# A float32 transformer layer on one core: the order of two subtractions in the gate units, and two output tiles moved to the end in halves

## The chip, the cores and the metric

The kernel runs on one core of one Trainium2 chip. The metric is the device time of one execution in microseconds. An execution's own time is a little longer than its span in the profile, which runs from its first to its last instruction.

## The reference, cut to what matters

One layer on 512 tokens of width 1024, all in float32: a feed-forward block, a token mixer (two kinds of attention), a second feed-forward block, and a final norm. The change lies in the two feed-forward blocks and in the final norm.

```python
def rmsnorm(x, g):
    y = x32 * lax.rsqrt(jnp.mean(x32 * x32, axis=-1, keepdims=True) + EPS)
    return y * g

def swiglu(x, w_gate, w_up, w_down):          # d_ff is 2816
    return (jax.nn.silu(x @ w_gate) * (x @ w_up)) @ w_down

x = x + 0.5 * swiglu(rmsnorm(x, ffn1_norm), ...)
x = x + token_mixer(rmsnorm(x, mix_norm), ...)
x = x + 0.5 * swiglu(rmsnorm(x, ffn2_norm), ...)
return rmsnorm(x, final_norm)
```

## The kernel before

**Layout.** Everything is transposed: x is eight tiles x0 to x7 of 128 features by 512 tokens. A "half" is 256 tokens, `left` or `right`. To keep float32 precision each operand is split into a high part (a cast to fp32r, on ScalarE) and a low part (the rest, by a subtraction on VectorE), and each product is three matmuls: high x high, high x low, low x high (`mm3`, lines 123 to 125 of the profile).

**Units and steps.** The two blocks are called a and b in tile names (`pygb` is bank y of a gate unit in block b). Most of a block is a list `units`, worked in order:

- `g` and `u`: two rows of gate (or up) columns at once, by a seven-product scheme after Strassen and Winograd. Its steps, in the order of `SEVEN`, are `a11` to bank w, `s3` to z, `s2` to x, `a12` to w, `s1` to y, `a22` to x, `s4` to y. A step is 12 matmuls, 256 wide.
- `p`: a plain product of one output tile with the first six rows of the activations (`PLAIN`), 18 matmuls 512 wide, added to x.
- `d`: a down unit, again seven steps, for two output tiles and eight rows; there are two groups of four.

In both blocks the list runs: gate and up units, five plain tiles (0 to 4), the first down group, more gate and up units, three plain tiles (5 to 7), the second down group. The final norm follows block b.

**Banks.** A step's partial sum is seeded from another bank (ScalarE copies w to x, then x to y). In a gate unit, after `s1`, bank y plus p7 (a half tile that ScalarE copied out of bank z into `res["bc"]`, called `rbc_n` in the profile) is one half of the second row; after `a22`, bank x plus p7 is the other. `s4` accumulates into bank y again, so it must come after the first of these adds. The adds are line 414 of the profile (`second_row`), and they write into tile `g1`; a Silu (line 495) follows in place. The first row comes from banks w and y by a Silu each (line 476) into tile `g0`. Both tiles are from a pool of two buffers (`ptb`), so a new pair's g0 and g1 take the buffers of the pair before.

**What happens to a finished pair.** After the up unit, `kept` forms the combinations that the down units need and splits them. The last two splits are `t0_rest` (h4 from g0 and h3) and `t1_rest` (h6 from g1 and h5), subtractions on VectorE, line 526. They are the last readers of the old g0 and g1.

**What sets the order.** On TensorE, VectorE and ScalarE the order is written out by hand, on SP and POOL too: the planner `pipeline` puts every small task on a heap with a due time and a rank. Due times are counted in `STEP` (1410 ns, one step) and `PLAIN_STEP` (4080 ns); tasks are issued in order of due time, rank and entry, and each engine works its own instructions strictly in that order. For a step at time t, its cast is due at t - 4 steps, its subtraction at t - 3 (line 386; `total`, lines 364 and 366, adds up two weights for `s2` and `s4`), its product at t. The results of a step are handled when the next starts.

**Weights.** `load` brings a unit's weight rows to one of three raw buffers through SP. `weight_sums` makes two sums of weight blocks: SP loads one block to a slot, and POOL issues a second, accumulating transfer on top. It is due 14 steps ahead, and not before the slot is free. In group 0 the down units use slots 8 to 11 in turn, in group 1 slots 8 to 11 and then 0 to 3.

**The end.** The last down unit (tiles 6 and 7) has `LAST_SEVEN`: steps `a22` and `s1` change places, so that the left halves of both tiles are done one step earlier. `last` squares the finished halves; `final_means` sums squares over features with one-column matmuls (line 1229) and makes the reciprocal root (lines 1232 to 1240); `final_spread` spreads the scale over partitions with a matmul (line 1244); `final_out` multiplies the eight tiles of a half by gain and scale (line 1254) and stores them, mostly in pairs (lines 1257, 1259). The left half's means stand ahead of the last step; its spread and one pair of outputs follow that step, then the right half's means, the other three left pairs, the right half's spread and its outputs.

Of the kernel before, what the change touches and what calls it, by code (L numbers as in the profile page):

```python
# [44 lines left out]

SEVEN = (("a11", "w", "b11"), ("s3", "z", "t3"), ("s2", "x", "t2"), ("a12", "w", "b21"),
         ("s1", "y", "t1"), ("a22", "x", "t4"), ("s4", "y", "b22"))
LAST_SEVEN = SEVEN[:4] + (SEVEN[5], SEVEN[4], SEVEN[6])

PAIR_SLOTS = ((6, 7, 16, 17, 18, 19, 20), (28, 29, 30, 31, 32, 33, 21),  # L50
              (34, 35, 36, 37, 38, 39, 40), (41, 42, 12, 13, 43, 14, 15))
GROUP_SUMS = (((8, 9), (10, 11), (8, 9), (10, 11)), ((8, 9), (10, 11), (0, 1), (2, 3)))


STEP, PLAIN_STEP = 1410, 4080
HS = S // 2
ODD = 8
F32_MAX = 3.4028234e38
# [6 lines left out]
def tile_macaron(ctx: ExitStack, tc, xs, xT, wf, wgu1, wst1, wd1, wdg1, wqk, wv, wo, wgu2, wst2, wd2,  # L65
# [132 lines left out]
    def ffn(wgu, wst, wd, wdg, n0, n1, norm, early, res, nm, hooks, ended, first=None,  # L198
# [96 lines left out]
        units = [("g", n1)]  # L295
        for j in range(n1 + 2, PLAIN + 8, 2):
            units += [("g", j), ("u", j)]
        units += [("p", m) for m in range(5)] + [("d", 0, m) for m in range(0, KD, 2)]
        for j in range(PLAIN + 8, JF, 2):
            units += [("g", j), ("u", j)]  # L300
        units += [("p", m) for m in range(5, KD)] + [("d", 1, m) for m in range(0, KD, 2)]
        ops, begin, starts, now = [], {}, [], 0
        for u in units:
            begin[u] = len(ops)
            seven = LAST_SEVEN if last is not None and u == units[-1] else SEVEN
            for o in (("p",),) if u[0] == "p" else seven:
                ops.append((u, o))
                starts.append(now)
                now += PLAIN_STEP if u[0] == "p" else STEP
        starts.append(now)  # L310

        def rows(u):
# [4 lines left out]

        def sum_slots(u):
            if u[0] == "d":
                return GROUP_SUMS[u[1]][u[2] // 2]  # L320
            if u == units[0]:
                return PAIR_SLOTS[0][:2]
            if u[1] == PLAIN + 8:
                return GROUP_SUMS[0][u[0] == "u"]
            o = 2 if u[0] == "g" else 4
            return PAIR_SLOTS[(u[1] - PLAIN) // 2 % 4][o:o + 2]

# [12 lines left out]

        def load(u):
            raws[u] = []
            whole = [wd[u[1]]] if u[0] == "p" else [rows(u)[0], rows(u)[1][:, 512:]]
            for a in whole:
                t = wp.tile([P, 1024], F32, tag="raw", name=f"raw{len(raws[u])}{nm}{u[0]}")
                nc.sync.dma_start(t[:, :a.shape[-1]], a)
                raws[u].append(t)

        def source(t):
            u, o = ops[t]  # L350
            r0 = raws[u][0]
            if o[0] == "p":
                return r0[:, :PLAIN * P]
            return {"a11": r0[:, :512], "a12": r0[:, 512:], "a22": raws[u][-1][:, :512],
                    "s1": sums[u][0][:], "s3": sums[u][1][:], "s2": second.get(u),
                    "s4": second.get(u)}[o[0]]
# [10 lines left out]

        def high(t):
            u, o = ops[t]
            if o[0] == "p":  # L370
                half.clear()
                h, l = w_place()
                made[t] = h[:, :PLAIN * P], l[:, :PLAIN * P]
            else:
                if not half:
                    h, l = w_place(ODD)
                    half.extend([(h[:, :512], l[:, :512]), (h[:, 512:], l[:, 512:])])
                    if t and ops[t - 1][1][0] == "p":

                        half.pop(0)  # L380
                made[t] = half.pop(0)
            A.copy(made[t][0], source(t))  # L382
# [41 lines left out]

        def product(t):
            u, o = ops[t]
            h, l = made.pop(t)
# [13 lines left out]
            banks = made[u]  # L441
            seeded = o[0] not in ("a11", "s3")
            for p, mv in enumerate(moving(u, o[2])):
                c = slice(p * P, (p + 1) * P)
                mm3(banks[o[1]], h[:, c], l[:, c], *mv, not seeded and p == 0, p == 3, seeded)


            if o[0] == "a11":
                put(starts[t + 1], A.copy, banks["x"], banks["w"])
            elif o[0] == "s2":  # L450
                put(starts[t + 1], A.copy, banks["y"], banks["x"])
            elif u[0] == "d":
                down_step(starts[t + 1], u, o[0], banks)
            else:
                pair_step(starts[t + 1], u, o[0], banks)

        def bank_tags(u):


            seq = [v for v in units if v[0] != "p"]  # L460
            n = seq.index(u)
            return ("mm",) * 4 if n == 0 or n % 2 else ("s", "t", "t", "s")

        def pair_step(t, u, o, banks):
# [4 lines left out]
            def tile(r):  # L469
# [3 lines left out]
                return g[j][r]  # L473

            def silu(r, c, p):
                A.activation(tile(r)[:, c], p, AF.Silu)

            def second_row(c, p):
                add(tile(1)[:, c], p, p7)

            def times_up(r, c):
                mul(g[j][r][:, c], ups[j + r][:, c], g[j][r][:, c])
# [1 line left out]
            if o == "s3":  # L484
                put(t, A.copy, p7, pz)
            elif u[0] == "g":
                if o == "a12":
                    put(t, silu, 0, left, pw)
                    if j == n1:
                        put(t + STEP, times_up, 0, left)  # L490
                elif o == "s1":
                    put(t, second_row, right, py)
                elif o == "a22":
                    put(t, second_row, left, px)
                    put(t + STEP * (j > n1), lambda: A.activation(
                        g[j][1][:], g[j][1][:], AF.Silu, scale=-1.0))
                elif o == "s4":
                    put(t, silu, 0, right, py)
                    if j == n1:
# [16 lines left out]
        def kept(j, t1, t0, t2):  # L516
# [64 lines left out]
            put(n + 2 * STEP, t0_parts)  # L581
            put(n + 2 * STEP, stt, g1[:, right], g1[:, right], -1.0, g0[:, left], ALU.subtract)
            put(n + 2 * STEP, stt, g1[:, left], g1[:, right], -1.0, g1[:, left], ALU.subtract)
            put(n + 3 * STEP, t0_rest)

            at(n + 3 * STEP, 5, t1_parts)
            put(n + 4 * STEP, t1_rest)

        def down_step(t, u, o, banks):
            _, group, m = u  # L590
# [15 lines left out]
            if last is not None and u == units[-1]:  # L606
                last(t, o, put)
            elif group == 1 and o in ("a22", "s4"):
                ended(m + (o == "a22"), t, put)

        def pipeline():
            seen = {}
            for t, (u, o) in enumerate(ops):
                if o[0] == "p":
# [3 lines left out]
                else:  # L618
                    if t == begin[u]:
                        if u != units[0]:  # L620

# [13 lines left out]
                    at(starts[t] - 3 * STEP, 2.5, low, t)  # L635
                at(starts[t], 4, product, t)
            if bias is not None:
                at(starts[begin["p", 5]], 5, bias[0])
# [563 lines left out]
    root = sp.tile([P, 1], F32, tag="root", name="root", bufs=1)  # L1202
    fin = {}

    def last(t, o, put):


        left, right = slice(0, HS), slice(HS, S)
        if o == "s3":
            fin["sq"] = [slot(4 + i, f"sql{i}") for i in range(2)]  # L1210
        q6, q7 = fin["sq"]
        for name, n, q, c in (("a12", KD - 2, q6, left), ("a22", KD - 1, q7, left),
                              ("s1", KD - 1, q7, right), ("s4", KD - 2, q6, right)):
            if o == name:
                put(t, A.activation, q[:, c], x[n][:, c], AF.Square)
        if o == "s3":
            put(t, A.activation, root[:], eps[:], AF.Sqrt)
        elif o == "s1":
            put(t, final_means, 0)
        elif o == "s4":  # L1220
            put(t, final_end)

    def final_means(hh):
        ps = pp.tile([P, S], F32, tag="mm", name=f"st_n4{hh}", bufs=4)
        n = NQ // 2
        for i in range(n):
            c = slice((hh * n + i) * P, (hh * n + i + 1) * P)
            for q, src in enumerate((sq, *fin["sq"])):
                T.matmul(ps[:, i:i + 1], src[:, c], ones_d[:, 0:1], start=q == 0, stop=q == 2)
        y = sp.tile([P, n], F32, tag="ly", name=f"ly{hh}")  # L1230
        t = sp.tile([P, n], F32, tag="lt", name=f"lt{hh}")
        A.activation(y[:], ps[:, :n], AF.Sqrt, bias=eps[:])
# [27 lines left out]
                    out[2 * g2 * P:(2 * g2 + 2) * P, c].rearrange("(m p) q -> p m q", p=P), y2)  # L1260

    def final_end():
        final_spread(0)
        final_out(0, range(1))
        final_means(1)
        final_out(0, range(1, 4))
        final_spread(1)
        final_out(1, range(4))

    n3 = {}  # L1270
# [102 lines left out]
```

## Time and profile before

| | us |
|---|---|
| median of 3 runs | 961.75 (961.2 to 962.27) |
| profiled execution, its own time | 961.41 |
| its span | 959.6 |
| TensorE matmuls busy | 937.5 |
| VectorE busy | 725.1 |
| ScalarE busy | 535.6 |
| granted TensorE clock, mean | 0.993 |

The page adds up each engine's busy time; the views of waits and timelines say which instruction stood still and what ended its wait. A timeline row is start, duration, engine, line, operation, tiles and shape; where the engine sat idle before, the length and the releaser follow in brackets. The end of a matmul is modelled, so the distance of matmul starts is the better measure of TensorE's pace. VectorE and ScalarE overlap instructions a little, so there too the distance of starts is what one costs in a row: a 128x512 instruction of VectorE lasts 0.68 us in its row and the next starts 0.60 us later.

### The profile page before, as it was taken

To read this page: it belongs to the slowest core of one execution; us is meant where nothing else is said; L and a number is where in the kernel's file an instruction comes from. 1 tells how busy PE (TensorE), PEld (TensorE's weight loads), DVE (VectorE), ACT (ScalarE), POOL (GpSimd) and SP (SyncE) were. 2 spreads that over 40 slices of the span, in tenths; PEclk is the share of its full clock that TensorE was granted. 3 is DMA by queue.
4 is the path that set the end of the run, shared out by engine and by line. 5 is a ranking of instruction groups with operands and counts; after the bars stand their busy time and mean duration, and the time that the engine had idled before them with its cause. 6 is when DMAs were issued, how large, how long until landed. Compare 5 with 4: busy or idle time off the path is not lost.

```text
span 959.6 us, 17173 instructions
## 1 busy us (share of the span) xinstructions
PE 937.5 (98%) x6452; PEld 867.9 (90%) x6452; DVE 725.1 (76%) x1490; ACT 535.6 (56%) x1102; POOL 98.4 (10%) x117
## 2 busy tenths in 40 slices
PE   9999999999999999999999999999999999999995
PEld 7789998999999998988989888889999899999995
DVE  7697887677887896669764547697888677787786
ACT  7455664455664665566756555455666345666462
POOL 0011101012102100000000003110120111220100
PEclk9999999999999999999999999999999999999997
DMA  7175646578756732444232204454773757874732
GB/s 250 60 207 142 155 125 174 138 195 202 186 139 174 195 116 77 133 132 116 83 115 84 69 19 132 132 164 99 184 182 88 201 138 186 221 185 119 185 106 88
DMA packets 60388, 136.71 MB, mean 142 GB/s; under 512 B 6848, under 2 KB 9152, under 8 KB 60304
## 3 DMA queue, kind: packets, MB, share of 16 engines
q1 hardware_dynamic: 46304, 110.14, 35.0%
q0 software_dynamic: 14000, 25.47, 17.0%
q8 instruction: 50, 0.82, 0.4%
q14 instruction: 34, 0.28, 0.1%
HBM read 130.30 MB, written 2.14 MB: 138 GB/s over the span
## 4 chain that ended last, share of the span: by engine, by line
PE 80%; DVE 15%; issue 2%; ACT 1%; DVEq 0%; POOL 0%; POOLq 0%
DVE w L386 5%; PE po L1040 2%; PE pua L123 1%; PE pua L124 1%; PE pua L125 1%; PE pwo L123 1%; PE pwo L124 1%; PE pwo L125 1%; PE pv L900 1%; PE pv L898 1%; PE pv L899 1%; PE pt L1027 1%; PE pq L123 1%; PE pq L125 1%; PE pq L124 1%
## 5 line engine op out<-in xcount | busy, mean ns | idle before, releaser
L1006 DVE CUSTOM_DVE_ANT_0 pr<-sc,strip 128x128 f32<-128x128 f32 (+3 forms) x64 | 30.9, 488 | 35.1 <-PE sc L1004 34.6
L1009 ACT ACTIVATE pr<-pr,mx 128x128 f32<-128x128 f32 (+3 forms) x64 | 36.0, 563 | 31.8 <-DVE mx L1006 30.9
L382 ACT CAST w<-s2b 128x512 fp32r<-128x512 f32 x50 | 31.1, 622 | 21.5 <-DVE s2b L364 19.8
L382 ACT CAST w<-s2a 128x512 fp32r<-128x512 f32 x46 | 28.6, 623 | 22.6 <-DVE s2a L364 19.6
L386 DVE TENSOR_TENSOR w<-s2b,w 128x512 fp32r<-128x512 f32 x50 | 34.2, 685 | 7.9 <-ACT w L382 7.9
L1040 PEld LDWEIGHTS po<-v,ptb 128*128 128x128 f32 x240 | 32.7, 191 | 5.3 <-ACT ptb L1030 2.7
L150 POOL TENSOR_TENSOR sq<-sq,sqt 128x512 f32<-128x512 f32 x7 | 10.9, 1562 | 254.7 <-ACT sqt L149 254.7
L386 DVE TENSOR_TENSOR w<-s2a,w 128x512 fp32r<-128x512 f32 x46 | 31.4, 683 | 6.5 <-ACT w L382 6.5
L898 PE MATMUL pv<-w,xh 128*128 128x256 f32 x128 | 36.2, 283 | 0.0
L900 PE MATMUL pv<-w,xh 128*128 128x256 f32 x128 | 36.2, 283 | 0.0
L899 PE MATMUL pv<-w,xl 128*128 128x256 f32 x128 | 36.2, 282 | 0.0
L1040 PE MATMUL po<-v,ptb 128*128 128x64 f32 (+1 forms) x240 | 32.5, 269 | 1.8 <-ACT ptb L1030 1.7
L1030 ACT COPY ptb<-pt 128x128 f32<-128x128 f32 (+3 forms) x48 | 20.1, 425 | 20.2 <-PE pt L1027 19.9
L123 PE MATMUL pq<-xh,w 128*128 128x512 f32 x64 | 26.9, 421 | 0.0
L123 PE MATMUL pwo<-mh,w 128*128 128x512 f32 x64 | 26.0, 407 | 0.0
L124 PE MATMUL pwo<-ml,w 128*128 128x512 f32 x64 | 25.5, 398 | 0.0
L125 PE MATMUL pwo<-mh,w 128*128 128x512 f32 x64 | 25.5, 398 | 0.0
L124 PE MATMUL pq<-xl,w 128*128 128x512 f32 x64 | 25.1, 392 | 0.0
L123 PE MATMUL pk<-xh,w 128*128 128x512 f32 x64 | 25.1, 392 | 0.0
L125 PE MATMUL pq<-xh,w 128*128 128x512 f32 x64 | 25.1, 392 | 0.0
L125 PE MATMUL pk<-xh,w 128*128 128x512 f32 x64 | 25.0, 391 | 0.0
L124 PE MATMUL pk<-xl,w 128*128 128x512 f32 x64 | 25.0, 390 | 0.0
(661 smaller groups left out, 3994.1 us busy)
## 6 DMA issues: line engine op xcount, KB each, us to landing
raw_qk<-wqk_dram SPq DMA_DIRECT2D x16, 512.0 KB, 3.3
raw0bg<-wst_dram SPq DMA_DIRECT2D x9, 512.0 KB, 5.1
raw_gua<-wgu_dram SPq DMA_DIRECT2D x8, 512.0 KB, 3.9
raw0ag<-wst_dram SPq DMA_DIRECT2D x8, 512.0 KB, 4.6
raw0ad<-wdg_dram SPq DMA_DIRECT2D x8, 512.0 KB, 4.7
strip<-bias_rows SPq DMA_DIRECT2D x16, 256.0 KB, 3.6
raw_v<-wv_dram SPq DMA_DIRECT2D x8, 512.0 KB, 3.3
raw_wo<-wo_dram SPq DMA_DIRECT2D x8, 512.0 KB, 3.2
```

Of the source, the lines that this page charges most:

```text
L123: T.matmul(po, wh, mh, start=first, stop=False, skip_group_check=on)
L124: T.matmul(po, wh, ml, start=False, stop=False, skip_group_check=on)
L125: T.matmul(po, wl, mh, start=False, stop=last, skip_group_check=on)
L382: A.copy(made[t][0], source(t))
L386: V.tensor_tensor(l, source(t), h.bitcast(F32), op=ALU.subtract)
L898: T.matmul(po, xh[k][:, xs], wh[:, o:o + 256], start=k == 0, stop=False)
L899: T.matmul(po, xl[k][:, xs], wh[:, o:o + 256], start=False, stop=False)
L900: T.matmul(po, xh[k][:, xs], wl[:, o:o + 256], start=False, stop=k == KD - 1)
L1006: V.tensor_tensor_reduce(out=pi, in0=ps[:, :w], in1=st["b"][m][:, w - 1::-1], op0=ALU.add, op1=ALU.min, scale=1.0, scalar=3.0e38, accum_ou ...
L1009: A.activation(pi, pi, AF.Exp, scale=-1.0, bias=st["mx"][:, m, i:i + 1], accum_out=st["ls"][:, m, i:i + 1])
L1030: A.copy(ptb[:, :w], pt[:, :w])
L1040: T.matmul(st["po3"][:, i, d0:d0 + dn], st["ptb", m, i][:, k * P:(k + 1) * P], vt[u // 4, k][:, fo + d0:fo + d0 + dn], start=k == 0, stop= ...
```

## The change

**Gate units, both blocks.** The two adds of the second row write into `res["bc"]` in place of `g1`, and the Silu reads it from there into `g1`. The first half of the first row's Silu is due one step later (not for a block's first gate unit). `t0_rest` and `t1_rest` are due two steps later for every pair but a block's first, with a rank that puts them behind a step's own results. On VectorE this gives, in a gate unit that follows an up unit: subtraction for `raw0`, first add, h4, subtraction for `s3`, second add, h6. Before, h4 and h6 stood four and two subtractions and sums ahead of the first add.

**Block b alone.** Plain tiles 3 and 4 go to the second group of plain tiles (so three come before each down group). Plain tiles 6 and 7 go to the end, behind the second down group, in four half products of 18 matmuls 256 wide: left of 6, left of 7, right of 6, right of 7. Their split weights are kept from the left to the right half. The last down unit has the common order `SEVEN`. All down units use slots 8 to 11.

**The end.** Squares are taken per half tile after each half product; those of tile 6 are added to the running sum. The left half's means stand inside the right half of tile 6, ahead of its last three matmuls. Its spread and first pair of outputs stand inside the right half of tile 7, ahead of its last six. After the last product come the right half's means, two left pairs, the reciprocal root, the right half's spread, the last left pair and the right half's outputs.

```diff
-LAST_SEVEN = SEVEN[:4] + (SEVEN[5], SEVEN[4], SEVEN[6])
-GROUP_SUMS = (((8, 9), (10, 11), (8, 9), (10, 11)), ((8, 9), (10, 11), (0, 1), (2, 3)))
+GROUP_SUMS = ((8, 9), (10, 11))
-STEP, PLAIN_STEP = 1410, 4080
+STEP, PLAIN_STEP, HALF_STEP = 1410, 4080, 2130
...
-        units += [("p", m) for m in range(5)] + [("d", 0, m) for m in range(0, KD, 2)]
+        plain = 5 if last is None else 3
+        units += [("p", m) for m in range(plain)] + [("d", 0, m) for m in range(0, KD, 2)]
...
+        units += [("p", m) for m in range(plain, KD if last is None else KD - 2)]
+        units += [("d", 1, m) for m in range(0, KD, 2)]
+        if last is not None:
+            units += [(h, m) for h in "lr" for m in (KD - 2, KD - 1)]
...
+        def half_product(t, m, o):
+            c = left if o == "l" else right
+            h, l = made[t] if o == "l" else made[t - 2]
+            po = mm_bank(f"p{o}{nm}{m}")
+            for k in range(PLAIN):
+                w = slice(k * P, (k + 1) * P)
+                mm3(po[:, :HS], h[:, w], l[:, w], ah[k][:, c], al[k][:, c],
+                    k == 0, k == PLAIN - 1)
+                last(starts[t], m, o, k, put)
+            put(starts[t + 1], stt, x[m][:, c], po[:, :HS], 0.5, x[m][:, c], ALU.add)
+            last(starts[t + 1], m, o, PLAIN, put)
...
                 if o == "a12":
-                    put(t, silu, 0, left, pw)
                     if j == n1:
+                        put(t, silu, 0, left, pw)
                         put(t + STEP, times_up, 0, left)
+                    else:
+                        at(t + STEP, 2, silu, 0, left, pw)
                 elif o == "s1":
-                    put(t, second_row, right, py)
+                    put(t, add, res["bc"][:, right], py, p7)
                 elif o == "a22":
-                    put(t, second_row, left, px)
-                    put(t + STEP * (j > n1), lambda: A.activation(
-                        g[j][1][:], g[j][1][:], AF.Silu, scale=-1.0))
+                    put(t, add, p7, px, p7)
+                    put(t + STEP * (j > n1), silu, 1, slice(0, S), res["bc"][:], -1.0)
...
-            put(n + 3 * STEP, t0_rest)
             at(n + 3 * STEP, 5, t1_parts)
-            put(n + 4 * STEP, t1_rest)
+            late = 2 * STEP * (j > n1)
+            at(n + 3 * STEP + late, 1, t0_rest)
+            at(n + 4 * STEP + late, 1, t1_rest)
...
+    def last(t, m, o, k, put):
+        hh = int(o == "r")
+        c = slice(hh * HS, (hh + 1) * HS)
+        if k == PLAIN:
+            q = fin.setdefault("sq", {})
+            if m not in q:
+                q[m] = slot(8 + m - (KD - 2), f"sql{m}")
+            put(t, A.activation, q[m][:, c], x[m][:, c], AF.Square)
+            if m == KD - 2:
+                put(t, lambda: V.tensor_tensor(sq[:, c], sq[:, c], q[m][:, c], op=ALU.add))
+            if (o, m) == ("r", KD - 1):
+                put(t, final_end)
+        elif (o, m, k) == ("l", KD - 2, 0):
+            A.activation(root[:], eps[:], AF.Sqrt)
+        elif (o, m, k) == ("r", KD - 2, PLAIN - 2):
+            final_means(0)
+            final_rstd(0)
+        elif (o, m, k) == ("r", KD - 1, PLAIN - 3):
+            final_spread(0)
+            final_out(0, range(1))
...
     def final_end():
-        final_spread(0)
-        final_out(0, range(1))
         final_means(1)
-        final_out(0, range(1, 4))
+        final_out(0, range(1, 3))
+        final_rstd(1)
         final_spread(1)
+        final_out(0, range(3, 4))
         final_out(1, range(4))
```

More of the change, by code (lines that the diff above doesn't have):

```diff
@@ L297, in ffn @@
             units += [("g", j), ("u", j)]
-        units += [("p", m) for m in range(5)] + [("d", 0, m) for m in range(0, KD, 2)]
+        plain = 5 if last is None else 3
+        units += [("p", m) for m in range(plain)] + [("d", 0, m) for m in range(0, KD, 2)]
         for j in range(PLAIN + 8, JF, 2):
             units += [("g", j), ("u", j)]
-        units += [("p", m) for m in range(5, KD)] + [("d", 1, m) for m in range(0, KD, 2)]
+        units += [("p", m) for m in range(plain, KD if last is None else KD - 2)]
+        units += [("d", 1, m) for m in range(0, KD, 2)]
+        if last is not None:
+            units += [(h, m) for h in "lr" for m in (KD - 2, KD - 1)]
         ops, begin, starts, now = [], {}, [], 0
@@ L304, in ffn @@
             begin[u] = len(ops)
-            seven = LAST_SEVEN if last is not None and u == units[-1] else SEVEN
-            for o in (("p",),) if u[0] == "p" else seven:
+            for o in ((u[0],),) if u[0] in "plr" else SEVEN:
                 ops.append((u, o))
                 starts.append(now)
-                now += PLAIN_STEP if u[0] == "p" else STEP
+                now += {"p": PLAIN_STEP, "l": HALF_STEP, "r": HALF_STEP}.get(u[0], STEP)
         starts.append(now)
@@ L319, in sum_slots @@
             if u[0] == "d":
-                return GROUP_SUMS[u[1]][u[2] // 2]
+                return GROUP_SUMS[u[2] // 2 % 2]
             if u == units[0]:
@@ L323, in sum_slots @@
             if u[1] == PLAIN + 8:
-                return GROUP_SUMS[0][u[0] == "u"]
+                return GROUP_SUMS[u[0] == "u"]
             o = 2 if u[0] == "g" else 4
@@ L342, in load @@
             raws[u] = []
-            whole = [wd[u[1]]] if u[0] == "p" else [rows(u)[0], rows(u)[1][:, 512:]]
+            whole = [wd[u[1]]] if u[0] in "pl" else [rows(u)[0], rows(u)[1][:, 512:]]
             for a in whole:
@@ L351, in source @@
             r0 = raws[u][0]
-            if o[0] == "p":
+            if o[0] in ("p", "l"):
                 return r0[:, :PLAIN * P]
@@ L369, in high @@
             u, o = ops[t]
-            if o[0] == "p":
+            if o[0] in ("p", "l"):
                 half.clear()
-                h, l = w_place()
+                h, l = w_place(ODD * (o[0] == "l"))
                 made[t] = h[:, :PLAIN * P], l[:, :PLAIN * P]
@@ L426, in product @@
             u, o = ops[t]
+            if o[0] in ("l", "r"):
+                half_product(t, u[1], o[0])
+                return
             h, l = made.pop(t)
@@ L455, in product @@
                 pair_step(starts[t + 1], u, o[0], banks)
+        def half_product(t, m, o):
[9 more added lines that the diff above has]
+            last(starts[t + 1], m, o, PLAIN, put)
         def bank_tags(u):
-            seq = [v for v in units if v[0] != "p"]
+            seq = [v for v in units if v[0] not in "plr"]
             n = seq.index(u)
@@ L467, in pair_step, with silu @@
             p7 = (sq if u[0] == "u" else res["bc"])[:, left]
-            def tile(r):
+            def silu(r, c, p, scale=1.0):
                 if r not in g.setdefault(j, {}):
                     g[j][r] = tp.tile([P, S], F32, tag="ptb", name=f"g{r}{nm}{j}")
[L473 to L479, printed above, removed]
+                A.activation(g[j][r][:, c], p, AF.Silu, scale=scale)
             def times_up(r, c):
@@ L605, in down_step @@
                 put(t, stt, x0_[:, right], py, 0.5, x0_[:, right], ALU.add)
-            if last is not None and u == units[-1]:
-                last(t, o, put)
-            elif group == 1 and o in ("a22", "s4"):
+            if group == 1 and o in ("a22", "s4") and (last is None or m < KD - 2):
                 ended(m + (o == "a22"), t, put)
@@ L613, in pipeline @@
             for t, (u, o) in enumerate(ops):
-                if o[0] == "p":
+                if o[0] in ("p", "l"):
                     at(starts[t] - 2 * PLAIN_STEP, 1, load, u)
@@ L617, in pipeline @@
                     at(starts[t] - 2 * STEP, 2.5, low, t)
-                else:
+                elif o[0] != "r":
                     if t == begin[u]:
@@ L637, in pipeline @@
             if bias is not None:
-                at(starts[begin["p", 5]], 5, bias[0])
+                at(starts[begin["p", plain]], 5, bias[0])
                 at(starts[begin["d", 1, 0] + 2], 5, bias[1])
@@ L1203, in tile_macaron @@
     fin = {}
[L1205 to L1221, printed above, removed]
+    def last(t, m, o, k, put):
[18 more added lines that the diff above has]
+            final_out(0, range(1))
     def final_means(hh):
@@ L1227, in final_means, with final_rstd @@
             c = slice((hh * n + i) * P, (hh * n + i + 1) * P)
-            for q, src in enumerate((sq, *fin["sq"])):
-                T.matmul(ps[:, i:i + 1], src[:, c], ones_d[:, 0:1], start=q == 0, stop=q == 2)
+            for q, src in enumerate((sq, fin["sq"][KD - 1])):
+                T.matmul(ps[:, i:i + 1], src[:, c], ones_d[:, 0:1], start=q == 0, stop=q == 1)
+        fin["ps", hh] = ps
+    def final_rstd(hh):
+        ps, n = fin["ps", hh], NQ // 2
         y = sp.tile([P, n], F32, tag="ly", name=f"ly{hh}")
```

## The prediction

> **What bounds the kernel now.** I read the page first, then TensorE's waits, then the chain that ended last, then the timelines of TensorE, VectorE and ScalarE where the chain leaves TensorE.
>
> ```profile
> span 959.6 us, 17173 instructions
> PE 937.5 (98%) x6452; PEld 867.9 (90%) x6452; DVE 725.1 (76%) x1490; ACT 535.6 (56%) x1102; POOL 98.4 (10%) x117
> ```
>
> TensorE is the bound; only what it issues, and the time it stands still, counts. Its waits (engine, tile and line, releaser; total, times, longest):
>
> ```profile
> PE pyga L123 <- DVE g1a L414: 3.9, 6, 1.3
> PE pygb L123 <- DVE g1b L414: 3.1, 6, 0.5
> ```
>
> Six times in each block the step `s4` of a gate unit waits for VectorE's add L414, which reads bank y after step `s1`. `s4` accumulates into that bank, so the add must have read it first; between the two lies only step `a22`. The longest such place of the second block, on TensorE and then on VectorE:
>
> ```profile
> 696.85 0.28 PE L125 MATMUL pxgb<-ttb,w 128*128 128x256 f32 x1
> 697.65 0.39 PE L123 MATMUL pygb<-xh,w 128*128 128x256 f32 x1 [0.52 <-DVE g1b L414]
> ...
> 694.17 0.69 DVE L526 TENSOR_TENSOR h4b<-g0b,h3b 128x512 fp32r<-128x512 f32 x1
> 694.77 0.69 DVE L386 TENSOR_TENSOR w<-s2b,w 128x512 fp32r<-128x512 f32 x1
> 695.37 0.68 DVE L526 TENSOR_TENSOR h6b<-g1b,h5b 128x512 fp32r<-128x512 f32 x1
> 695.98 0.68 DVE L364 TENSOR_TENSOR s2b<-s1bu,raw0bu 128x512 f32<-128x512 f32 x1
> 696.58 0.68 DVE L386 TENSOR_TENSOR w<-raw0bu,w 128x512 fp32r<-128x512 f32 x1
> 697.18 0.42 DVE L414 TENSOR_TENSOR g1b<-pygb,rbc_n 128x256 f32<-128x256 f32 x1
> ```
>
> Matmuls of this width start every 0.118 us, so a start 0.80 us after the last is 0.68 us lost (the bracket's 0.52 leaves out the modelled end of the last matmul). VectorE starts a 512-wide instruction every 0.60 us without a gap: it isn't waiting, it is behind, and h4 and h6, which nothing needs soon, stand ahead of the add. The first such place of the first block is longer:
>
> ```profile
> 102.96 0.28 PE L125 MATMUL pxga<-tta,w 128*128 128x256 f32 x1
> 104.56 0.39 PE L123 MATMUL pyga<-xh,w 128*128 128x256 f32 x1 [1.33 <-DVE g1a L414]
> ...
> 102.27 0.69 DVE L386 TENSOR_TENSOR w<-raw0au,w 128x512 fp32r<-128x512 f32 x1
> 103.29 0.69 DVE L526 TENSOR_TENSOR h6a<-g1a,h5a 128x512 fp32r<-128x512 f32 x1 [0.33 <-ACT h5a L564]
> 104.08 0.42 DVE L414 TENSOR_TENSOR g1a<-pyga,rbc_n 128x256 f32<-128x256 f32 x1
> ```
>
> Here 1.60 - 0.12 = 1.48 us are lost. All twelve: 1.48 + 11 x 0.68 = 8.96 us, the whole of what can be won in the gate units. Then the end, on VectorE:
>
> ```profile
> 945.05 0.17 DVE L1233 RECIPROCAL ly<-ly 128x2 f32<-128x2 f32 x1 [1.10 <-ACT ly L1232]
> 946.31 0.42 DVE L423 SCALAR_TENSOR_TENSOR x<-pydb,x 128x256 f32<-128x256 f32 x1
> 948.84 0.17 DVE L1233 RECIPROCAL ly<-ly 128x2 f32<-128x2 f32 x1 [0.78 <-ACT ly L1232]
> 950.09 2.43 DVE L1254 SCALAR_TENSOR_TENSOR y<-x,x,bcl 128x256 f32<-128x256 f32 x6
> 952.83 2.82 DVE L1254 SCALAR_TENSOR_TENSOR y<-x,x,bcl 128x256 f32<-128x256 f32 x7
> ```
>
> TensorE's last product ends at 946.25; 13.35 us follow in which 14 of the 16 output multiplies (0.39 us each) run, six of them for the left half after the right half's scale chain.
>
> **The gate units.** The order of the changed kernel's instructions on VectorE shows h4 behind the first add and h6 behind the second. In the pair above the add would start 2 x 0.60 earlier, at 695.98, and end at 696.40; TensorE could issue `s4` at 696.97. The add's own input, bank y after `s1`, is complete near 695.65 (`s4`'s natural start less one step of 1.42 us, plus the 0.16 by which a matmul outlasts its slot). So the wait goes, with 0.5 us to spare: 11 x 0.68 = 7.48 us. In the first pair only h6 moves: the add starts at 102.87, ends at 103.29, against a natural `s4` at 103.08; of 1.48 some 0.25 remain, 1.2 gained. Sum 8.7. Bounds: 8.96 if that pair clears too; 7.5 if a tenth of a us stays in each place.
>
> What is late next? h4 now delays ScalarE's first-row Silu, which refills g0's buffer and stands one step later in its queue, and h6 the second-row Silu, which refills g1's. For that reason the adds now write in place into the spread tile. Behind the Silus in ScalarE's queue are the casts for the next up unit: s2's would run near 697.3 (696.69 before) and s1's near 699.4 (699.65 before). VectorE's subtractions behind these come at 698.5 and 700.3, and TensorE wants s1's half only at the up unit's fifth step, 696.97 + 5 x 1.42 = 704.1: about 3 us cover. VectorE idled 0.73, 0.73 and 1.22 us in the rest of that pair, so it doesn't fall behind when pairs come 0.68 us sooner. I cost these moves at nothing; without that cover each us would be paid once per unit (rival 4).
>
> **Plain tiles 3 and 4 moved to the second group.** Product, load, cast and subtraction go together. The first down group then follows three plain tiles instead of five, as the second did before, and there TensorE waited for nothing. The weight sums of the second group go back to slots 8 to 11 (slots 0 to 3 still hold activations); the first group used these slots in that very turn, and its SP loads and POOL's accumulating loads (issue to landing 4.4 to 6.4 us) held nobody up. Zero; the lower bound is zero as well, since no wait is there to be won.
>
> **Two tiles in halves.** 512-wide plain matmuls start every 0.225 us (759.77 to 760.67 for four), 256-wide ones every 0.118: per tile 36 x 0.118 - 18 x 0.225 = +0.20, for two +0.4. Bound: nothing to +0.6. [...]
>
> **The end, replayed from rows.** Time 0 is the start of the right half of tile 6. Five of its six inner steps take 1.77 us; its mean matmuls are 8 passes instead of 12 (12 took 943.33 to 944.58), 0.83 us. They need the left half of tile 7, added and squared 1.1 us after its last product, so they don't wait. Square root to finished diagonal is 1.63 us (944.76 to 946.39), done at 4.4; TensorE reaches the spread inside tile 7's right half at 4.4 and spends 0.53 on it. Last product ends at 5.87. Against before TensorE issues +0.4 - 0.42 + 0.53 = +0.5 us. On VectorE the right half of x6, its square and the sum, then two outputs come first, so the right half of x7 starts at 6.35, 0.4 late. From there: square ends 7.2, means and root 8.3, diagonal 9.65, spread readable 10.45 (946.45 to 947.19 before); four left outputs fit beside the means and two beside the spread; eight right outputs end at 13.67. The last store ended 3.95 us after the last output before (955.65 to 959.6), so 17.6, which is 11.75 after the last product against 13.35. Net: -1.6 + 0.5 = -1.1 us. Bounds: 0 (x7's chain waits a further us) to -2.2 (VectorE reaches x7 in time, halves cost nothing).
>
> **Sum.** -8.7 - 1.1 = -9.8 us. The profiled execution took 961.41 us with a span of 959.6; its span should come to 949.8 and its time to 951.6. The median of the runs is 0.34 above it: 951.9. The bounds of the terms, -7.5 and 0 against -8.96 and -2.2, give 950.6 to 954.3; run-to-run spread (961.2 to 962.3) puts a half on either side.
>
> **Rivals.**
> 1. *Half the wait is replaced.* Something not seen by me (the in-place adds, a Silu on ScalarE) keeps the add or `s4` late by 0.3 to 0.4 us per pair: -9.8 + 4.3 = 956.2. For it: VectorE is busy 17.7 of the 21 us from 687 to 708. Against: half a us of slack. Chance 0.12.
> 2. *The gate order gives nothing*, because an add of another place becomes the last; only the end is won: 960.7. The trace shows no second wait of TensorE in these units. Chance 0.04.
> 3. *Narrow halves are bound by weight loads*: at the 0.19 us of one LDWEIGHTS row, 72 halves cost 72 x 0.19 - 36 x 0.225 = +5.6, so 957.1 with the rest. Against: the down steps load a weight per matmul too and start every 0.118. [...] Chance 0.04.
> 4. *Slower: ScalarE's queue.* In 15 gate units Silus now stand behind h4 and h6, with the casts of the up unit behind them. If this puts s1's cast late by more than its 3 us of cover, each further us is paid 15 times; from 3.65 us per unit the 9.8 are eaten, at 4 us late the time is 952 + 15 = 967. By the rows h4 and h6 come 2.2 and 2.5 us later than now, into time in which ScalarE idles, and s1's cast stays near 699.4. Chance 0.04.
>
> **Numbers.** The forecast has 0.76. Its own range, 950.1 to 954.8, holds about 0.72; to leave out no more than 2 in 10 the range goes up into rival 1, to 955.8, and on the low side to 950.0. This kernel's runs can tell about 0.2% (1.9 us) from no change. Faster by more: forecast, rivals 1 and 3, 0.92. Within it: rival 2, 0.04. Slower: rival 4, 0.04.
>
> **What would show it.** In the profile after: no `pyga` or `pygb` wait left among TensorE's waits but a short one near 103 us; gate-and-up pairs 20.0 us apart instead of 20.67; the add right behind the subtraction for raw0, h4 behind it. Casts and Silus on ScalarE in the places named. At the end, 256-wide `plb` and `prb` matmuls every 0.118 us, x7's last add about 0.5 us after its product, eight outputs after the last spread, 11 to 12 us from last product to end. A new wait of TensorE on a weight tile, or pairs still 20.6 us apart, would prove the forecast wrong.

## The result, and the profile after

| | before | after |
|---|---|---|
| median of the runs (four each) | 961.48 us (959.84 to 962.27) | 949.57 us (948.38 to 951.25) |
| ratio, 95% interval | 1 | 0.988 (0.9859 to 0.990) |
| profiled execution | 961.41 us | 949.0 us |
| its span | 959.6 us | 947.2 us |
| last product's end | 946.2 us | 935.3 us |
| from there to the end | 13.4 us | 11.9 us |

The kernel became faster, by 12.4 us between the profiled executions where 9.8 were forecast; the median lies 0.4 us below the forecast's range. Before the last product 10.9 us were won, behind it 1.5.

The head of the page after, and then the rows of TensorE's waits that belong to the end and to the gate units (engine, tile, line, releaser; total, times, longest):

```profile
span 947.2 us, 17265 instructions
PE 932.4 (98%) x6480; PEld 867.0 (92%) x6480; DVE 725.2 (77%) x1494; ACT 533.3 (56%) x1102; POOL 98.3 (10%) x117
```

```profile
PE bcl L1266 <- DVE dgl L1262: 1.7, 1, 1.7
...
PE st_n L1247 <- ACT sql L413: 1.1, 1, 1.1
...
PE pyga L122 <- DVE rbc_n L416: 0.2, 1, 0.2
```

The two rows of six waits are gone. One wait of `pyga`, 0.2 us, stands for the first pair. The same place of the second block as the prediction showed, on TensorE (start, duration, instruction), with the step before `s4` in the first row:

```profile
690.34 0.28 PE L124 MATMUL pxgb<-ttb,w 128*128 128x256 f32 x1
690.46 0.28 PE L122 MATMUL pygb<-xh,w 128*128 128x256 f32 x1
690.58 0.28 PE L123 MATMUL pygb<-xl,w 128*128 128x256 f32 x1
```

`s4` starts 0.12 us behind `a22`, as the 256-wide matmuls around it do, and the next 0.12 later again. On VectorE the adds stand where they were forecast, each right behind one subtraction, with h4 and h6 after them:

```profile
688.87 0.68 DVE L388 TENSOR_TENSOR w<-raw0bu,w 128x512 fp32r<-128x512 f32 x1
689.47 0.41 DVE L416 TENSOR_TENSOR rbc_n<-pygb,rbc_n 128x256 f32<-128x256 f32 x1
689.80 0.68 DVE L540 TENSOR_TENSOR h4b<-g0b,h3b 128x512 fp32r<-128x512 f32 x1
690.40 0.68 DVE L388 TENSOR_TENSOR w<-s3bu,w 128x512 fp32r<-128x512 f32 x1
691.00 0.41 DVE L416 TENSOR_TENSOR rbc_n<-pxgb,rbc_n 128x256 f32<-128x256 f32 x1
691.34 0.68 DVE L540 TENSOR_TENSOR h6b<-g1b,h5b 128x512 fp32r<-128x512 f32 x1
```

The first add ends at 689.88, 0.58 us ahead of `s4`: the slack of half a us in the prediction. The first pair of the first block, on TensorE and VectorE:

```profile
102.97 0.27 PE L124 MATMUL pxga<-tta,w 128*128 128x256 f32 x1
103.47 0.39 PE L122 MATMUL pyga<-xh,w 128*128 128x256 f32 x1 [0.23 <-DVE rbc_n L416]
103.69 0.28 PE L123 MATMUL pyga<-xl,w 128*128 128x256 f32 x1
...
103.00 0.42 DVE L416 TENSOR_TENSOR rbc_n<-pyga,rbc_n 128x256 f32<-128x256 f32 x1
```

Here the add starts at 103.00, not 102.87, and 0.38 us of standing still is left (0.25 forecast). Note the third TensorE row: it starts 0.22 behind the second, not 0.12.

ScalarE, whose queue rival 4 feared:

```profile
690.60 0.39 ACT L490 ACTIVATE g0b<-pwgb 128x256 f32<-128x256 f32 x1 [2.15 <-DVE h4b L540]
692.91 0.61 ACT L384 CAST w<-s1bu 128x512 fp32r<-128x512 f32 x1
```

The first-row Silu does wait for h4, 2.15 us, and s1's cast comes 2.45 us behind `s4`, as in the forecast (2.43). TensorE shows no wait on a weight tile from it. The end, on VectorE:

```profile
935.79 0.42 DVE L425 SCALAR_TENSOR_TENSOR x<-prb,x 128x256 f32<-128x256 f32 x1
937.87 0.17 DVE L1255 RECIPROCAL ly<-ly 128x2 f32<-128x2 f32 x1
940.53 0.48 DVE L1276 SCALAR_TENSOR_TENSOR y<-x,bcl 128x256 f32<-128x256 f32 x1 [0.53 <-PE bcl L1266]
940.93 2.83 DVE L1276 SCALAR_TENSOR_TENSOR y<-x,x,bcl 128x256 f32<-128x256 f32 x7
```

x7's last add starts 0.47 us after its product (0.48 forecast), and eight outputs, not fourteen, remain.

One difference lies where the change did nothing, in the token mixer between the two blocks. Before, TensorE stands still there for 1.7 us, and the profile's stretches behind it show its clock (columns: stretch; its length; busy us and count of PE, PEld, DVE, ACT, POOL; granted clock; DMA share; GB/s):

```profile
547.49:549.49 2.00, 1.58 (x11) 1.50 (x12) 0.96 (x3) 1.50 (x3) 0.00 (x0) 1.00 0.00 0
549.49:552.90 3.41, 3.41 (x12) 2.82 (x11) 1.59 (x7) 0.92 (x4) 0.00 (x0) 0.50 0.39 136
552.90:554.90 2.00, 2.00 (x14) 1.73 (x14) 0.49 (x2) 0.56 (x1) 0.00 (x0) 1.00 0.08 31
```

After, the stand-still is there too (1.7 us, `po` behind `ptb`), but the clock stays whole:

```profile
543.00:545.00 2.00, 2.00 (x13) 1.82 (x14) 1.42 (x4) 1.07 (x2) 0.00 (x0) 1.00 0.00 0
545.00:547.00 2.00, 2.00 (x13) 1.69 (x12) 1.06 (x5) 0.88 (x4) 0.00 (x0) 1.00 0.17 33
547.00:549.00 2.00, 2.00 (x14) 1.78 (x13) 0.95 (x5) 1.04 (x3) 0.00 (x0) 1.00 0.58 229
```

TensorE's steps over that stretch are 1.5 us longer before than after. So the 10.9 us ahead of the last product, by TensorE's steps, are 9.7 in the gate units, 1.5 in the mixer, and -0.3 in the rest (the halves and the spread). The question for the runs: where do the 1.0 us in the gate units beyond the forecast and the 1.5 us in the mixer come from?

### The profile page after: what moved, and what is told of

Same layout as the page of the kernel before. It is cut to its first block, busy times and chain, and to the rows that moved or that the text cites. A ratio compares the mean times of both kernels' runs of the same rounds, so it can differ in the third digit from the quotient of the medians.

```text
span 947.2 us, 17265 instructions
## 1 busy us (share of the span) xinstructions
PE 932.4 (98%) x6480; PEld 867.0 (92%) x6480; DVE 725.2 (77%) x1494; ACT 533.3 (56%) x1102; POOL 98.3 (10%) x117
## 4 chain that ended last, share of the span: by engine, by line
PE 92%; DVE 5%; ACT 2%; issue 1%; DMA 0%; DVEq 0%
PE po L1053 2%; PE pua L122 1%; PE pua L123 1%; PE pua L124 1%; PE pwo L122 1%; PE pwo L123 1%; PE pwo L124 1%; PE pv L913 1%; PE pv L911 1%; PE pv L912 1%; PE pt L1040 1%; PE pq L122 1%; PE pq L124 1%; PE pq L123 1%; PE pda L123 1%; PE pda L124 1%
## 5 line engine op out<-in xcount | busy, mean ns | idle before, releaser
L149 POOL TENSOR_TENSOR sq<-sq,sqt 128x512 f32<-128x512 f32 x7 | 10.9, 1563 | 253.2 <-ACT sqt L148 253.2
```

## The experiments

The main theory (A in the expectations): a standing-still place costs its wait and a restart besides, since the first matmul after the wait is followed 0.23 us later instead of 0.118; and the mixer's 1.5 us are the clock of one execution, no effect of the change. The rivals put the gate units' extra gain on something else in the change, or the mixer's on the change itself. The first four kernels shared 21 runs of before (median 961.4 us, 959.75 to 962.21), the other four 15 runs (961.21, 959.49 to 961.9).

**The gate units alone.** The kernel before, with the order of the gate pair and the late `t0`, `t1` of the kernel after:

```diff
 before.py
-  put(t, second_row, right, py)
+  put(t, add, res["bc"][:, right], py, p7)
...
-  put(n + 3 * STEP, t0_rest)
-  put(n + 4 * STEP, t1_rest)
+  late = 2 * STEP * (j > n1)
+  at(n + 3 * STEP + late, 1, t0_rest)
+  at(n + 4 * STEP + late, 1, t1_rest)
```

> The gate units' new order alone, in both blocks; the units of block b and the end stay as before. Theory A (a place where TensorE stands still costs more than its wait: 0.68 us of wait and 0.10 us of a slow first matmul behind it): 12 places save 1.11 + 11 x 0.78 = 9.7 us, so the span is 949.9 where TensorE's clock is halved for 3.4 us in the mixer as in the profile of before, and 948.4 where it is not. Rival B (a place costs the 0.68 that I predicted, and the rest of the gain came out of the end): 8.7 us saved, 950.9. Rival C (the 1.5 us gained in the mixer belong to the change): 11.2 us saved whatever the clock did.

Measured: median 951.94, ratio 0.9909 (0.9896 to 0.9923), span 950.2. At the twelve places TensorE's steps are 9.7 us shorter than before: the first pair 1.10, each other place 0.67 to 0.68 of wait and 0.10 to 0.11 of restart. Its mixer is the one of before, and its clock falls in the same way:

```profile
544.55:547.96 3.41, 3.41 (x12) 2.83 (x11) 1.69 (x7) 0.77 (x4) 0.00 (x0) 0.50 0.37 112
```

So with the halved stretch on both sides the gate units alone give 9.4 us of span: 0.7 more than forecast for them, and nothing of it comes from the new end.

**The end alone.** The kernel after, with those two places as before:

```diff
 after.py
-  put(t, add, res["bc"][:, right], py, p7)
+  put(t, second_row, right, py)
...
-  at(n + 3 * STEP + late, 1, t0_rest)
+  put(n + 3 * STEP, t0_rest)
...
```

> The moved plain tiles and the halves at the end alone; the gate units keep the order of before. Theory A: TensorE issues 0.2 us more before its last product, and 1.5 us less lie behind it: -1.3 us, span 958.3 with the clock halved in the mixer, 956.8 without. Rival B: the end alone brings 2.2 us or more, 957.4 with the clock halved. Rival C: -1.3 and the mixer's 1.5 us come together only with the gate order, so nothing of the mixer here.

Measured: median 959.11, ratio 0.9978 (0.9969 to 0.9987), span 956.3. The twelve waits are back:

```profile
PE pyga L122 <- DVE g1a L416: 4.0, 6, 1.3
PE pygb L122 <- DVE g1b L416: 3.1, 6, 0.5
```

This profile has no halved stretch in the mixer (mean granted clock 0.997, in the profile of before 0.993), which is 1.6 of its 3.3 us; the end is worth 1.9, the start-up 0.2 the other way. That lies between the 1.3 of theory A and the 2.2 of rival B. In the kernel after the end's two parts came to 1.2 (1.5 less 0.3). Of the difference 0.5 us is one row, the last spread; first in the kernel after, then here:

```profile
939.27 1.22 PE L1266 MATMUL bcl<-dgl,ones_m 128*128 128x256 f32 x2 [1.73 <-DVE dgl L1262]
```

```profile
949.17 0.70 PE L1268 MATMUL bcl<-dgl,ones_m 128*128 128x256 f32 x2 [1.73 <-DVE dgl L1264]
```

In the kernel after TensorE's granted clock is 0.50 from 938.78 on, in the wait for the diagonal; here it is 1.00 from 945.00 to 950.28. Another 0.3 lies behind the last output: 3.48 us to the end of the span in the kernel after, 3.15 here. Theory A took the end from one profile that is long in both places. The product of the two ratios, 0.9909 x 0.9978 = 0.9887, is that of the whole change within its interval: the parts add up.

**The kernel after once more**, unchanged, for the clock in the mixer.

> The changed kernel once more. Theory A: 947.2 us span without a stretch of halved clock in the mixer, 948.7 with one; ratio to before 0.987 to 0.989. Rival C: always 947.2, since the mixer's gain belongs to the change.

Measured: median 950.14, ratio 0.9885 (0.9871 to 0.9898). The profiled run has a span of 946.9 and its mixer again at full clock:

```profile
545.00:547.00 2.00, 2.00 (x13) 1.71 (x12) 1.08 (x5) 0.88 (x4) 0.00 (x0) 1.00 0.24 41
```

Its other three runs have spans of 948.1 to 948.7, at a mean granted clock of 0.993 to 0.994 against 0.996. To judge by that and by their length they held the halved stretch, though only the profiled run's trace is kept. One kernel then shows both, 1.2 to 1.8 us apart, so the mixer's share of the difference isn't the change's.

**The kernel before, with the stand-still filled.** Eight matmuls of no use, into a tile that the next ones overwrite, are issued in the mixer where TensorE waits for `ptb`:

```diff
 before.py, values()
+  if (u, m, i) == (6, 1, NQ - 1):
+      for k in range(2 * NQ):
+          T.matmul(st["po3"][:, i, d0:d0 + dn], st["ptb", 0, i][:, k % NQ * P:(k % NQ + 1) * P],
+                   vt[u // 4, k % NQ][:, fo:fo + dn], start=True, stop=True)
```

> The kernel before with eight small matmuls, overwritten afterwards, where TensorE stands still for 1.7 us ahead of the last values product of unit 6 (545.9 to 547.9 us). Theory A: TensorE isn't idle there, its clock is not halved afterwards, and the span is 1.5 us shorter than the profile of before, 958.1; the gate waits stay. Rival C: the clock is not what differed; span 959.6, and the mixer's steps at 551 to 554 us as slow as before.

Measured: median 960.11, ratio 0.999 (0.9981 to 0.9999), span 958.8. TensorE at the place, and the stretches behind it:

```profile
546.53 1.89 PE L1041 MATMUL po<-v,ptb 128*128 128x64 f32 x16
548.39 1.10 PE L1044 MATMUL po<-v,ptb 128*128 128x64 f32 x8
```

```profile
548.00:550.00 2.00, 2.00 (x15) 1.81 (x15) 0.98 (x3) 1.48 (x3) 0.00 (x0) 1.00 0.00 0
550.00:552.00 2.00, 2.00 (x13) 1.68 (x12) 1.51 (x7) 0.45 (x3) 0.00 (x0) 1.00 0.08 10
```

Each of these matmuls counts twice in the records: the first row is the eight of no use, the second the four that the kernel wants. They start right behind the fill, and the clock stays whole; the steps there are 1.55 us shorter than in the profile of before. The span won only 0.8, since the first 12 us took 0.3 to 0.4 longer in this execution and 0.3 more passed behind the last output (4.27 us, 3.99 before). The runs say it more plainly than the profile: eleven runs at 959.51 to 960.61, where the 21 of before go from 959.75 up to 962.21. The upper part of that range is gone, the lower stays. The waits in the gate units remain at 3.9 and 3.2 us, so they aren't tied to the clock.

Why the same stand-still is followed by a halved stretch in one execution and not in another no run shows. Of the ten profiles five have the stretch (before, the gate units alone, and three runs below: h4 ahead, in place alone, x7's add first), three have the stand-still of 1.7 us without it (the kernel after in both its profiles, the end alone), and two have the stand-still filled. In the traces of before and after the granted clock changes at times that lie whole multiples of 3.4133 us apart: before, its record begins at 6.77 us and it changes at 549.49, 552.90 and 948.85 us, which are 159, 1 and 116 such lengths apart; after, it begins at 6.95 us and changes at 938.78 us, 273 lengths later. Counted off in these lengths, the stand-still of before (546.21 to 547.91) lies whole in the one from 546.08 to 549.49, and the next runs at 0.50. That of after (541.26 to 542.95) lies across an edge at 542.84, 1.57 us of it ahead of the edge, and from there to 549.66 the clock is 1.00. That is one trace of each kind; no run put the stand-still at a chosen place.

**h4 ahead of the first add.** In the kernel after, `t0` at its old due time:

```diff
 after.py
-  at(n + 3 * STEP + late, 1, t0_rest)
+  at(n + 3 * STEP, 1, t0_rest)
```

> The changed kernel with h4 ahead of the first add again (t0_rest due as before; h6 stays behind). The add then ends 0.60 us later, at 690.49 in place of 689.89 in the pair where s4 could start at 690.46. Theory A (a wait of TensorE, however short, is followed by a first matmul that takes 0.10 us more): 0.03 of wait and 0.10 of restart, 0.13 in 11 places, 1.4 us more than the changed kernel. Rival D (the restart is paid only behind a long wait): 0.3 us more. Rival B of the first runs (no restart cost at all): 0.3 us more.

Measured: median 951.65, ratio 0.9905 (0.9891 to 0.9918), span 950.6. The place in the second block, on TensorE and VectorE:

```profile
692.97 0.28 PE L124 MATMUL pxgb<-ttb,w 128*128 128x256 f32 x1
693.17 0.39 PE L122 MATMUL pygb<-xh,w 128*128 128x256 f32 x1
693.39 0.29 PE L123 MATMUL pygb<-xl,w 128*128 128x256 f32 x1
...
692.70 0.42 DVE L416 TENSOR_TENSOR rbc_n<-pygb,rbc_n 128x256 f32<-128x256 f32 x1
```

The add ends at 693.12 and `s4` starts at 693.17, 0.20 behind `a22` instead of 0.12: a wait of 0.08 us, so short that no bracket tells of it. The matmul after it still comes 0.22 later. Over the eleven places the wait is 0.076 to 0.086 and the restart 0.104 to 0.108, 2.07 us in all. Theory A had 1.4, with the right restart and too small a wait (0.03); the others, without a restart, had 0.3. This profile holds the halved stretch in the mixer (545.41 to 548.83 us, granted clock 0.50), and 947.2 + 2.07 + 1.5 = 950.8 comes near its span of 950.6. The restart is real, and a wait of 0.08 us pays it in full.

**In place alone.** In the kernel after, `t0` and `t1` both at their old due times. The adds' target, the later Silu and the rank that puts the two behind a step's own results stay new:

```diff
 after.py
-  late = 2 * STEP * (j > n1)
+  late = 0
```

> The changed kernel with both subtractions at their due times of before; the adds still write into the spread tile and the Silu stands where the change put it. Theory A (the two subtractions ahead of the add are the cause): 11 places lose 0.68 + 0.10 again, 8.6 us more than the changed kernel, span 955.8 without halved clock in the mixer. Rival E (the adds waited for the old g1 buffer, and writing elsewhere is what freed them): the gain stays, 947.2.

Measured: median 959.14, ratio 0.9982 (0.9973 to 0.9991), span 956.4, with the halved stretch (mean granted clock 0.995). TensorE's waits, then the place in its timeline:

```profile
PE pygb L122 <- DVE rbc_n L416: 3.1, 6, 0.5
PE pyga L122 <- DVE rbc_n L416: 2.8, 6, 0.5
```

```profile
696.31 0.39 PE L122 MATMUL pygb<-xh,w 128*128 128x256 f32 x1 [0.53 <-DVE rbc_n L416]
696.53 0.28 PE L123 MATMUL pygb<-xl,w 128*128 128x256 f32 x1
```

All but the first pair's long wait is back, 0.68 to 0.69 and 0.10 at each place; in the first pair the rank alone moves h6. Writing into the spread tile frees nobody by itself: the order of h4 and h6 against the adds is the cause. Whether the late order would work with the adds still writing into `g1` no run tried. With the halved stretch theory A came to 957.3; the end is 0.9 shorter here (11.0 us from the last product, 11.9 in the kernel after), by a last spread at full clock and less time behind the last output.

**x7's add first.** In the new end the left half's first output stood ahead of x7's last add on VectorE. Here it comes after:

```diff
 after.py
-  elif (o, m, k) == ("r", KD - 1, PLAIN - 3): final_spread(0); final_out(0, range(1))
+  elif (o, m, k) == ("r", KD - 1, PLAIN - 3): final_spread(0)
...
-  final_out(0, range(1, 3))
+  final_out(0, range(2))
...
-  final_out(0, range(3, 4))
+  final_out(0, range(2, 4))
```

> The changed kernel with the first output pair of the left half behind the last add of x7, and the left outputs two pairs before the right half's reciprocal and two behind its diagonal. Theory A (VectorE's queue holds x7's add back by 0.45 us at the end): the add starts 0.05 us after its product's end, the right half's outputs start 0.25 us sooner, as two more left outputs now stand in front of them: span 946.95. Rival F (ScalarE or TensorE sets the end's chain): no change within 0.05 us from last product to end, 11.9 us.

Measured: median 949.88, ratio 0.9885 (0.9872 to 0.9899), span 948.1 with the halved stretch in the mixer (mean granted clock 0.994). VectorE at the end:

```profile
936.80 0.42 DVE L425 SCALAR_TENSOR_TENSOR x<-prb,x 128x256 f32<-128x256 f32 x1 [0.26 <-PE prb L124]
...
941.72 0.47 DVE L1275 SCALAR_TENSOR_TENSOR y<-x,bcl 128x256 f32<-128x256 f32 x1
942.11 2.82 DVE L1275 SCALAR_TENSOR_TENSOR y<-x,x,bcl 128x256 f32<-128x256 f32 x7
```

The add now waits for its product (ended at 936.76) instead of the other way round, and the right half's outputs start 4.96 us behind that product; after, 940.53 - 935.32 = 5.21. That is the 0.25 expected, but it hangs on the clock: in both these profiles the last spread ran at 0.50 (1.22 us for its two matmuls after, where the end alone has 0.70). In the two profiles that have the order of the kernel after and a spread at full clock, the end alone and in place alone, these outputs start 4.70 us behind the product. With the new order they start 4.95 behind it at full clock too (in the run below), because four left outputs stand ahead of them on VectorE. So the new order wins 0.25 us or loses as much. In the medians it can't be told from the kernel after.

**All three joined**: this end, the filled stand-still, and in the first pair `t0` one step later as well, so that h6 and h4 both stand behind their adds there.

```diff
 after.py, with the last edit and the fill
-  at(n + 3 * STEP + late, 1, t0_rest)
+  at(n + 3 * STEP + (late or STEP * (j >= PLAIN)), 1, t0_rest)
```

> The changed kernel with three things more: the outputs ordered as in the run above, eight small matmuls in the mixer where TensorE stood still for 1.7 us, and h4 of the first pair of block a behind the add too. Theory A: 0.25 us at the end, 0.38 + 0.10 at the first pair, and no halved clock in the mixer in any run: span 946.5, and its runs lie closer together than those of the changed kernel, around 948.3 us. Rival C: the filling brings nothing, runs scatter as before by 2 us, median 0.7 us below the changed kernel.

Measured: median 947.99, ratio 0.9869 (0.9854 to 0.9884), span 946.0. No `pyga` or `pygb` row is left among TensorE's waits; the longest are now the end's own:

```profile
PE bcl L1269 <- DVE dgl L1265: 1.7, 1, 1.7
...
PE st_n L1250 <- ACT sql L413: 0.7, 1, 0.7
```

Its four runs lie within half a us (947.79 to 948.26). It is the best of the versions: 1.6 to 2.1 us below the two medians of the kernel after, and below every one of its eight runs, though the intervals of the ratios overlap. By TensorE's steps the first pair is 0.5 of the 1.2 us between this profile and the first of the kernel after; at the end the right half's outputs start 0.26 sooner and 0.33 less passes behind the last one. In the medians the rest fits the clock that no longer falls in the mixer (1.00 from 541 to 549 us in this profile), but no run took that apart.

## Why the prediction was right, and where it was not

The mechanism came as forecast, but the gain was larger than the range allowed. The step that failed is the price of a place in the gate units, and beside it the base was taken from one profile without a look at its clock.

**Gate units: right cause, too small by 1.0 us.** h4 and h6 ahead of the add were the cause (shown by the two runs that put h4, and then both, back to their old due times), and the slack behind the add is 0.58 us. What failed is the step that makes a place's loss 0.80 - 0.12: I took the start of `s4` against the start of `a22` and stopped there. The very next row of before belongs to the price:

```profile
697.65 0.39 PE L123 MATMUL pygb<-xh,w 128*128 128x256 f32 x1 [0.52 <-DVE g1b L414]
697.88 0.28 PE L124 MATMUL pygb<-xl,w 128*128 128x256 f32 x1
```

0.23 us where such matmuls stand 0.118 apart: 0.10 to 0.11 more at each place, about 1.1 over the eleven. So the bound called "the whole of what can be won", 8.96, was no bound. The first pair won 1.11 where 1.2 were forecast: 0.38 of wait and 0.10 of restart are left of 1.58.

**Nothing new is late: right.** The Silu and s1's cast ran where the forecast put them, and pairs come 19.88 us apart (690.46 to 710.34; 20.0 forecast, without the restart). Rivals 1, 2 and 4 find nothing in the trace.

**Plain tiles moved, two in halves: right.** No wait on a weight or a sum, and the halves start every 0.118 us, which settles rival 3. TensorE's net cost ahead of the last product was 0.3, not 0.5.

**The end: right in sum, in part by luck.** 1.5 us won from the last product on, 1.6 forecast. The steps come in the order given, but two of their terms were off and made up for each other. The last output ends 8.44 us behind the last product (935.32 to 943.75), where the working has 7.80 (5.87 to 13.67): it took the spread's time from a row at full clock, and in the profile after the spread ran at 0.50. The time between the last output and the end of the span, held at 3.95 us, is 3.48 in the kernel after. It is 3.08 to 3.17 in the other six profiles with the new end, and 3.99 to 4.27 in the three with the old one. No run tried why.

**The base: not looked at.** The working compares one profiled execution with a forecast, and the one before held 1.5 us of halved clock; the one after did not. To judge by their spans, 24 of the 36 runs of before that the experiments shared had it (959.3 us and more) and 12 had not (957.7 to 958.7). The mixer's stretches, shown above, were there to read. Spans with the stretch on both sides are 959.6 and 948.1 to 948.7, so the change itself is worth about 11 us: 9.7 - 0.3 + 1.5 = 10.9. Of the 2.6 us between forecast and profile, 1.0 is the gate units, 0.1 the end with TensorE's share of it, and 1.5 the clock. The two medians of the kernel after, 949.57 and 950.14, stand on either side of the range's lower end; the missing restart alone would have brought the forecast to 950.8 and the range down by as much, around both. How the rest of the distance divides between the clock and the time behind the last output no run shows.

## What to carry to other kernels

Price a wait from start to start on the bounding engine, and go on until the matmuls stand at their usual distance again: the first gap behind the wait belongs to it (0.23 us here, where 0.118 is usual). Before a sum is set against one profiled execution, look through its granted clock for a stretch at half speed, and ask whether the other execution will have it too. In the queue of an engine that is behind, the order counts: what releases the bound engine goes ahead of what nobody waits for yet.

## What the runs showed of the hardware

- A restart: the 256-wide matmul that follows a wait of TensorE is itself followed 0.22 to 0.23 us later, against 0.118 in the stream, and this 0.10 us is as large behind 0.08 us of waiting as behind 0.68. A wait is not its only occasion: before, the 256-wide matmul behind the one-column matmuls of the means is followed 0.21 us later too (944.58 to 944.79). What causes it no run shows.
- A stand-still of 1.7 us in the mixer was followed by a stretch of 3.41 us at half of TensorE's granted clock in five of the eight profiles that hold it, at a cost of 1.5 us, and not in the other three. With the stand-still filled, neither of the two profiles has it (1.00 from 545 to 556 and from 541 to 549 us), and the fifteen runs of those two kernels lie within 1.1 and 0.5 us. In the traces of before and after the clock changes at whole multiples of 3.4133 us from the start of its record. What decides whether it falls behind a stand-still no run shows.
